# A two-layer decoder trunk on one core: the MLP in two phases, its down-projection in seven products

## The chip, the core and the metric

The kernel runs on one core of a Trainium2 chip. The core has a matrix engine (TensorE, PE in the profile; its weight loads are PEld), three engines for elementwise work (VectorE or DVE, ScalarE or ACT, GpSimd or POOL), and DMA queues that SyncE (SP) and ScalarE issue to. Data lie in DRAM, in SBUF (128 partitions) and in PSUM, where matmuls accumulate: eight banks of 128 x 512 floats. The metric is the device time of one execution in microseconds (us); lower is better.

## The reference

Two layers on a sequence of T = 1024 tokens and D = 1024 channels in float32. Layer 0 mixes tokens with dilated attention and a gated convolution, layer 1 with retention; each layer ends in a gated MLP of inner width 2816:

```python
def conv_glu_ffn(xn, w_up, conv_w, w_down):
    u = causal_dwconv(xn @ w_up, conv_w)      # width 3, over tokens; w_up: [1024, 5632]
    g, val = jnp.split(u, 2, axis=-1)
    return (jax.nn.silu(g) * val) @ w_down    # [2816, 1024]
...
x = x + conv_glu_ffn(rms_norm(x, ffn_norm[l]), ffn_w_up[l], ffn_conv_w[l], ffn_w_down[l])
```

## The kernel before

**Precision.** A matmul operand is split into two rounded parts, hi and lo (`split`, L99: ACT casts hi, then POOL or DVE subtracts lo = src - hi), and a product is three passes (`PASSES`): hi*hi, hi*lo, lo*hi. A tile `hl` holds a split weight block of 128 x 512; there are HL = 6 of them, and RAW = 3 buffers `raw` for blocks as loaded.

**The residual stream** `xb` stays in SBUF, token tile by token tile (8 tiles of 128 tokens). The normed, transposed input of a projection is `xc`: seven split tiles (three blocks and four combinations of blocks) that the seven-product scheme needs.

**Up-projection.** `strassen` (L200) computes two column blocks of 128, a gate block and its value block, with the Strassen-Winograd scheme: seven products of 12 matmuls (4 K tiles x 3 passes) of 512 columns instead of eight. The products accumulate in the `b` banks; ACT and DVE add them into `u1` and `u2`. Weight sums s1 to s4 are made by DVE (L237, L238) and POOL (L239, L258). POOL makes the lo parts of all seven weights.

**The MLP loop.** `ffn` goes over 22 blocks j. After the seven products of block j, `conv` (L707) applies the width-3 convolution (ACT L717, four DVE operations L720), SiLU (L724) and the gate product (L725), and splits the result into `h`. Block j of `h` is then one K tile of the down-projection: `down` (through `sweep`, L282) multiplies it with a row block of w_down for all 8 token tiles and adds every output tile from an `o` bank to `xb` (L289, L294). The tables `MIX` and `LAST_MIX` say how many token tiles of the down-projection of block j - 1 go after each product of block j: the two kinds of product alternate on PE.

**The norm between phases.** `Norming.play` follows `PLAN`, a string of steps: a sweep of two token tiles (s), inverse rms (q), normed rows (r), transposes (t), combination into `xc` (c) for a pair of tiles, and products of the next projection's first block (h). After layer 0's MLP the sweeps of this plan are the down-projection of the last block, 48 matmuls. The first block after a norm works in two passes of 256 columns.

**What sets the order.** The code is written in an order of emission; a scheduler then places instructions on the engines' queues, and each engine runs its own queue in order and waits on semaphores.

Of the kernel before, what the change touches and what calls it, by code (L numbers as in the profile page):

```python
# [13 lines left out]
P = 128  # L14
# [15 lines left out]
PLAN = "s0 q0 s1 q1 r0 t0 s2 q2 c0 r1 t1 s3 q3 c1 r2 t2 c2 r3 h3 t3 c3 h4"  # L30
PLAN_LATE = "t0 c0 s2 q2 t1 s3 q3 c1 r2 t2 c2 r3 t3 h3 c3 h4"
# [7 lines left out]
PAIRS = ((0, 2), (1, 3), (4, 6), (5, 7))  # L39
ORDER = tuple(t for p in PAIRS for t in p)  # L40
# [3 lines left out]
def _constants():  # L44
    """Arrays that depend on the shapes alone."""
# [23 lines left out]
def trunk(tc, a):  # L69
# [29 lines left out]
    def split(hi, lo, src, eng=None):  # L99
        """src = hi + lo, both rounded to float32r"""  # L100
        act.copy(hi, src)  # L101
        (eng or pool).tensor_tensor(lo, src, f(hi), ALU.subtract)  # L102
# [39 lines left out]
    def rsqrt_mean(out, ss, n, width):  # L142
        """out = (ss / n + EPS) ** -0.5"""
# [3 lines left out]
    def row_gains(g, parts):  # L147
        """A gain of the D channels on every partition, in two halves."""
# [11 lines left out]
    def normed(xt, r, g, xn):  # L160
        """xn = xt * r * g"""
# [5 lines left out]
    def turn(xn, h, bank):  # L167
        """Four of the eight [128, 128] blocks of xn, transposed."""
# [29 lines left out]
    def strassen(w, c1, c2, xc, fp, banks, out, spare=None):  # L198
# [16 lines left out]
        def half(u, i):  # L215
            return u.rearrange("p (a b t) -> p a b t", a=2, b=2)[:, ps_ : ps_ + 2 // np_, i, :]
# [13 lines left out]
        for n, bank in enumerate(banks):  # L230
            cols_, ps_ = slice(n * width, (n + 1) * width), n
            if n == 0:
# [8 lines left out]
                weights(12, a12)  # L241
                u1, u2 = fp.tile([P, T], "u", 4), fp.tile([P, T], "u", 4)
# [60 lines left out]
    # =============================== layer 0: even mixer ===============================  # L303
# [57 lines left out]
    def natural(w, c0, half, banks):  # L361
        """banks[t] = xnorm[tokens of tile 4*half + t] @ w[:, c0:c0+512]"""
# [655 lines left out]
```

## Time and profile before

| | |
|---|---|
| time, median of 3 runs | 2870.95 us (2869.23 to 2872.1) |
| span of the profiled execution | 2866.6 us; its own time is not given, the runs' median is 4.35 us longer than this span |
| busy | PE 2760.7 us (96%), DVE 1810.0 (63%), POOL 1552.6 (54%), ACT 1101.8 (38%) |
| DMA | 210.84 MB, 74 GB/s on average |

The span is the time from the first to the last instruction on the core. Busy time is a sum over instructions; matmuls overlap each other, so the duration of one in a list (some 395 ns) is longer than the distance between two. The chain of work that ended last shows those distances. "Idle before" and an arrow name what an engine waited for.

### The profile page before, as it was taken

Reading aid. Unit: us, or ns where it says so; the run is one execution under the profiler, and the core shown is the slowest. Engines: PE = TensorE matmul, PEld = TensorE weight load, DVE = VectorE, ACT = ScalarE, POOL = GpSimd, SP = SyncE. Lnnn points to the kernel's source line nnn. Section 1 sums busy time; section 2 is a strip of 40 time slices with the busy share of each in tenths; the row PEclk is TensorE's granted clock in tenths of the full one; section 3 lists DMA queues with packets and bytes.
Section 4 is the critical chain, followed back from the end, with each engine's and each line's share of the span. In section 5 each row is a group of like instructions: output and inputs, shape, how many; then the busy total and the mean of one; then the engine's idle time right before and its main releaser. Section 6 shows DMA issues by size and latency. Waiting matters only on the chain.

```text
span 2866.6 us, 34181 instructions
## 1 busy us (share of the span) xinstructions
PE 2760.7 (96%) x12513; PEld 2229.6 (78%) x12513; DVE 1810.0 (63%) x2670; ACT 1101.8 (38%) x1860; POOL 1552.6 (54%) x1185
## 2 busy tenths in 40 slices
PE   8999999789999999978999999999997999999998
PEld 6877777677888888867888877788876888888887
DVE  4256665876776776785222224888777767767767
ACT  4344443343343343343333333323334343343342
POOL 6711113356566566555666665555556666566563
PEclk9999999899999999988999999999999999999999
DMA  4310002011111111103333335444221111111112
GB/s 152 103 43 25 21 32 82 22 57 52 55 48 52 56 48 49 59 22 96 111 101 112 111 99 190 150 143 151 88 74 53 48 49 55 49 51 56 49 52 77
DMA packets 214988, 210.84 MB, mean 74 GB/s; under 512 B 10368, under 2 KB 162340, under 8 KB 214820
## 3 DMA queue, kind: packets, MB, share of 16 engines
q1 hardware_dynamic: 207900, 183.49, 20.1%
q10 hardware_dynamic: 6920, 25.17, 2.3%
q8 instruction: 98, 1.61, 0.2%
q14 instruction: 70, 0.57, 0.1%
HBM read 179.26 MB, written 29.36 MB: 73 GB/s over the span
## 4 chain that ended last, share of the span: by engine, by line
PE 79%; DVE 10%; POOL 4%; issue 3%; DMA 2%; ACT 1%; SPq 0%; ACTq 0%; POOLq 0%; DVEq 0%
PE b L210 43%; PE o L289 18%; PE u L419 5%; PE n L368 2%; PE u L368 2%; PE s L457 2%; POOL hl L102 2%; DVE xb L294 2%; PE pv L485 1%; PE u L289 1%; DVE u L164 1%; PE pt L497 1%; DMA raw<-in_ret_wo 1%; DVE s L800 1%; PE b L171 1%
## 5 line engine op out<-in xcount | busy, mean ns | idle before, releaser
L210 PE MATMUL b<-xc,hl 128*128 128x512 f32 (+1 forms) x5676 | 1331.9, 393 | 6.1 <-DVE xc L102 2.8
L210 PEld LDWEIGHTS b<-xc,hl 128*128 128x128 f32 x5676 | 1056.3, 189 | 259.9 <-DVE xc L102 3.6
L102 POOL TENSOR_TENSOR hl<-raw,hl 128x512 fp32r<-128x512 f32 x435 | 576.8, 1332 | 881.8 <-ACT hl L101 846.0
L294 DVE TENSOR_TENSOR xb<-xb,o 128x512 f32<-128x512 f32 x880 | 571.3, 682 | 304.8 <-PE o L289 301.8
L101 ACT CAST hl<-raw 128x512 fp32r<-128x512 f32 x444 | 274.2, 619 | 794.5 <-issue 288.1
L289 PE MATMUL o<-hl,h 128*128 128x512 f32 x2112 | 520.6, 398 | 14.3 <-DVE xb L294 10.5
L289 PEld LDWEIGHTS o<-hl,h 128*128 128x128 f32 x2112 | 400.1, 190 | 113.0 <-DVE xb L294 15.0
L102 POOL TENSOR_TENSOR hl<-s,hl 128x512 fp32r<-128x512 f32 x260 | 408.0, 1570 | 108.1 <-ACT hl L101 107.8
L720 DVE SCALAR_TENSOR_TENSOR u<-u,cc,u 128x1023 f32<-128x1023 f32 (+3 forms) x184 | 289.2, 1580 | 7.9 <-ACT u L717 5.0
L101 ACT CAST hl<-s 128x512 fp32r<-128x512 f32 x269 | 165.7, 618 | 88.4 <-PE b L210 40.2
L271 DVE TENSOR_TENSOR u<-u,b 128x512 f32<-128x512 f32 (+1 forms) x68 | 45.9, 675 | 212.5 <-issue 190.5
L419 PE MATMUL u<-xT,hl 128*128 128x512 f32 x576 | 164.5, 408 | 0.0
L237 DVE TENSOR_TENSOR s<-raw,raw 128x512 f32<-128x512 f32 x68 | 54.4, 800 | 130.9 <-DMA raw<-in_ffn_w_up 35.0
L258 POOL TENSOR_TENSOR s<-raw,s 128x512 f32<-128x512 f32 x65 | 124.9, 1921 | 5.1
L717 ACT ACTIVATE u<-u,cc 128x1024 f32<-128x1024 f32 (+1 forms) x92 | 102.0, 1115 | 56.7 <-DVE u L273 31.7
L239 POOL TENSOR_TENSOR s<-raw,raw 128x512 f32<-128x512 f32 x65 | 89.0, 1370 | 51.4 <-DMA raw<-in_ffn_w_up 43.6
L419 PEld LDWEIGHTS u<-xT,hl 128*128 128x128 f32 x576 | 99.2, 189 | 21.8 <-issue 5.8
L102 POOL TENSOR_TENSOR h<-u,h 128x512 fp32r<-128x512 f32 x84 | 106.6, 1288 | 0.0
L289 PE MATMUL o<-hl,ya 128*128 128x512 f32 x384 | 98.0, 406 | 3.7 <-DVE xb L294 3.7
L289 PEld LDWEIGHTS o<-hl,ya 128*128 128x128 f32 x384 | 73.2, 193 | 21.4 <-DVE xb L294 4.6
L725 DVE TENSOR_TENSOR u<-u,u 128x1024 f32<-128x1024 f32 (+1 forms) x46 | 56.2, 1222 | 50.5 <-ACT u L724 50.5
L102 POOL TENSOR_TENSOR xc<-u,xc 128x512 fp32r<-128x512 f32 x48 | 67.8, 1442 | 36.5 <-ACT xc L101 33.1
(183 smaller groups left out, 3078.2 us busy)
## 6 DMA issues: line engine op xcount, KB each, us to landing
raw<-in_ffn_w_up SPq DMA_DIRECT2D x176, 256.0 KB, 2.8
scr<-u ACTq DMA_DIRECT2D x48, 512.0 KB, 4.2
raw<-in_ffn_w_down SPq DMA_DIRECT2D x88, 256.0 KB, 2.6
raw<-in_even_w_in SPq DMA_DIRECT2D x72, 256.0 KB, 2.8
raw<-in_ret_wo SPq DMA_DIRECT2D x64, 256.0 KB, 2.6
xb<-in_x SPq DMA_DIRECT2D x16, 512.0 KB, 5.0
raw<-in_ret_wv SPq DMA_DIRECT2D x32, 256.0 KB, 4.1
raw<-in_ret_wg SPq DMA_DIRECT2D x32, 256.0 KB, 3.3
```

The source lines that it names most:

```text
L101: act.copy(hi, src)
L102: (eng or pool).tensor_tensor(lo, src, f(hi), ALU.subtract)
L210: pe.matmul(u, hl[:, ws, k * P : (k + 1) * P], xc[b][:, xs, k, cols_], start=(first and k == 0 and i == 0), stop=(k == 3 and i == 2), skip ...
L239: helper.tensor_tensor(s3, a11, a21, ALU.subtract)
L258: helper.tensor_tensor(s4, a12, s2, ALU.subtract)
L289: pe.matmul(o, lhs[j](ls, t), ws[j][hf][:, w, :], start=(j == 0 and i == 0), stop=(j == n - 1 and i == 2),)
L294: dve.tensor_tensor(xs, xs, o, ALU.add)
L368: pe.matmul(banks[t], xT[:, xs, k, t0 : t0 + P], hl[:, ws, :], start=(k == 0 and i == 0), stop=(k == KT - 1 and i == 2),)
L419: pe.matmul(u, hl(ws, k), xT[:, xs, k, hf * 512 : (hf + 1) * 512], start=(k == 0 and i == 0), stop=(k == KT - 1 and i == 2),)
L457: pe.matmul(sp[:, :n], qk[h0 : h0 + 64, 0, qs, i * P : (i + 1) * P], qk[h0 : h0 + 64, 1, ks, k0 : k0 + n], start=(j == 0), stop=(j == 2),)
L717: act.mul(c[:, t0:t1], u[:, t0:t1], wcol(2, jj))
L720: dve.scalar_tensor_tensor(c[:, s0:t1], u[:, s0 - d : t1 - d], wcol(2 - d, jj), c[:, s0:t1], ALU.mult, ALU.add)
```

## The change

The MLP becomes two phases. In the first the 22 blocks of the up-projection follow each other without products of the down-projection between them; `conv` leaves its result unsplit, and ACT's queue stores it to a DRAM tensor `hs`. In the second, `down_steps` computes the down-projection as Strassen-Winograd on tokens x inner width x channels, each halved: seven products of 11 K tiles x 4 token tiles x 3 passes. Their accumulators are the four `o` banks (x) and the four `b` banks (y). Six stages of 11 steps follow each other:

- stage 1: h11 x w11 into x, which is then added to the left half of tiles 0 to 3 and kept;
- stage 2: h12 x w21 into y;
- stage 3: two products of sums (s1, t1 into y, s2, t2 onto x), 24 matmuls a step; POOL also makes h11 - h21;
- stage 4: two more (s4 x w22 onto y, (h11 - h21) x t3 onto x), 24 matmuls a step;
- stage 5: h22 x t4 onto half of x, 6 matmuls a step; t4 is also stored to DRAM (`ts`);
- stage 6: the other half of the same product, 6 matmuls a step, from `ts` and `hs`; the norm that follows runs beside stages 5 and 6 (`PLAN_DOWN`).

Blocks of h come back from `hs`, are kept in `q` tiles in the space of `xc`, and are split anew in the phase (POOL or DVE). `RAW` becomes 5, `HL` 7, the norm's gains get two buffers `g` of their own, and retention's token halves become 0 to 511 and 512 to 1023 (`lay=1`, `PAIRS[1]`).

```diff
-RAW = 3
-HL = 6
+RAW = 5
+HL = 7
+KH = NFF // 2
+AHEAD = 3
+PLAN_DOWN = (
+    "a0 d2 a1 d2 a2 d2 a3 d5 A0 A1 b0 b1 B0 B1",
+    "d3 t0 c0 d3 t1 c1 d3 h1 d2 b2 A2 B2 b3 h1 t2 c2 h2 A3 B3 t3 c3 h4",
+)
-MIX = (0, 0, 0, 0, 3, 3, 2)
-LAST_MIX = (0, 0, 0, 0, 3, 0, 0)
...
+            if space is None:
+                kw["reuse_waits"] = "tile"
...
-            self.g = row_gains(g, [wk.tile([P, HALF], "s", 3) for _ in range(2)])
+            self.g = row_gains(g, [wk.tile([P, HALF], "g", 2) for _ in range(2)])
...
+    def down_steps(w):
...
+        def plain(k, l, r):
+            return [(hilo(l), hilo(r, None, dve))]
...
+        def load_56(k):
+            q["22", k] = lhs(1, 1, k)
+            r = u_tile()
+            sync.dma_start(out=r, in_=w[k * P : (k + 1) * P, :])
+            return lhs(1, 0, k, raw()), q["22", k], r[:, :HALF], r[:, HALF:], rhs(1, 1, k)
+
+        def make_56(k, a21, a22, b11, b12, b22):
+            s1, t1 = add(s_tile(), a21, a22, ALU.add), add(s_tile(), b12, b11, ALU.subtract)
+            p5 = hilo(s1), hilo(t1)
+            q["s2", k] = s2 = add(tile(), s1, q["11", k], ALU.subtract)
+            q["t2", k] = t2 = add(tile(), b22, t1, ALU.subtract)
+            add(q["11", k], q["11", k], a21, ALU.subtract, pool)
+            return [p5, (hilo(s2, None, dve), hilo(t2, None, dve))]
...
+        def make_37(k, b22, b12):
+            s4, t3 = add(q["12", k], q["12", k], q["s2", k], ALU.subtract), add(s_tile(), b22, b12, ALU.subtract)
+            return [(hilo(s4, None, dve), hilo(b22)), (hilo(q["11", k]), hilo(t3, None, dve))]
...
+        def make_4(k, b21):
+            t4 = add(q["t2", k], b21, q["t2", k], ALU.subtract)
+            r = quarter(q["22", k][:, :256]), hilo(t4, None, dve)
+            act.dma_start(out=ts[k], in_=t4)
+            return [r]
+
+        def load_4b(k):
+            t4, a22 = raw(), raw()
+            sync.dma_start(out=t4, in_=ts[k])
+            sync.dma_start(out=a22[:, :256], in_=hs[KH + k, :, HALF + 256 : T])
+            return t4, a22
...
+        groups = (
+            (load_1, plain, [(x, four, True)], lambda: evict(x, 0, 0)),
+            (load_2, plain, [(y, four, True)], lambda: evict(y, 0, 0)),
+            (load_56, make_56, [(y, four, True), (x, four, False)], lambda: (evict(y, 4, 1), evict(x, 0, 1))),
+            (load_37, make_37, [(y, four, False), (x, four, False)], lambda: (evict(y, 0, 1), evict(x, 4, 1))),
+            (load_4, make_4, [(x[:2], two, False)], lambda: evict(x[:2], 4, 0)),
+            (load_4b, make_4b, [(x[2:], two, False)], lambda: evict(x[2:], 6, 0)),
+        )
...
+        for j in range(NFF):
...
+            for n, _ in enumerate(steps):
+                if n == 2:
+                    store()
+                if j == NFF - 1 and n >= 1:
+                    if n == 1:
+                        close_xc(0, 1)
+                        d.append(down_steps(w_down))
+                    advance(1)
...
+            held.append((j, conv(j, us)))
+        advance(4)
+        store()
+        tail(until, d[0])
...
+    def to_ret(until, down):
+        until(4)
+        nrm = Norming(a["odd_norm"][0:1], 1)
+        nrm.play(PLAN_DOWN[0], sweep=down)
+        open_xc()
...
+        nrm.play(PLAN_DOWN[1], nxt["xc"], down, nxt["head"][0])
```

Where instructions stand, before and now (the number at a name's end is its buffer's). First PE, inside the MLP of layer 0, in a block of the up-projection; `b` are the seven products' banks, `o` the down-projection's. Before, from the fourth product of a block to the end of the block:

```order
L210 MATMUL b_6973<-xc_4914,hl_7006 128x512 x12
L210 MATMUL b_6976<-xc_4913,hl_7021 128x512 x12
L289 MATMUL o_7058<-hl_6943,h_6928 128x512 x3
L289 MATMUL o_7063<-hl_6948,h_6928 128x512 x3
...
L289 MATMUL o_7083<-hl_6948,h_6928 128x512 x3
L210 MATMUL b_6973<-xc_4915,hl_7039 128x512 x12
L289 MATMUL o_7103<-hl_6943,h_6928 128x512 x3
```

Now, the same place and the next block's start:

```order
L218 MATMUL b_6254<-xc_4916,hl_6287 128x512 x12
L218 MATMUL b_6257<-xc_4915,hl_6302 128x512 x12
L218 MATMUL b_6254<-xc_4917,hl_6321 128x512 x12
L218 MATMUL b_6257<-xc_4914,hl_6337 128x512 x12
L218 MATMUL b_6400<-xc_4912,hl_6380 128x512 x12
```

The 48 matmuls of the down-projection have left the block, and the seven products of one block stand directly before those of the next.

Then DVE in stage 3 of the down-projection (layer 0), about one step; `q` are kept blocks, `s` sums, L741 is `add`, L109 the lo part of a split:

```order
L741 TENSOR_TENSOR s_9254<-raw_9111,q_9107 128x512
L109 TENSOR_TENSOR hl_9174<-q_9168,hl_9174 128x512
L741 TENSOR_TENSOR q_9264<-s_9254,q_8580 128x512
L741 TENSOR_TENSOR s_9256<-u_9109 128x512
L741 TENSOR_TENSOR q_8830<-q_8830,q_9264 128x512
L741 TENSOR_TENSOR q_9266<-raw_9113,s_9256 128x512
L109 TENSOR_TENSOR hl_9216<-q_9211,hl_9216 128x512
```

Before, what DVE did for the down-projection was the addition of its tiles to `xb`, between the convolution's steps:

```order
L294 TENSOR_TENSOR xb_71<-xb_71,o_7843 128x512
L294 TENSOR_TENSOR xb_71<-xb_71,o_7848 128x512
L720 SCALAR_TENSOR_TENSOR u_7887<-u_7692,cc_5382,u_7887 128x1023
L720 SCALAR_TENSOR_TENSOR u_7887<-u_7692,cc_5382,u_7887 128x1022
L276 TENSOR_TENSOR u_7691<-u_7691,b_7696 128x2x256
```

Seven operations a step on SBUF operands alone have come (the fifth is stage 4's s4, which the scheduler has moved into stage 3), and the 16 additions from PSUM per block are gone; four per group of banks remain at the stages' ends.

Last PE at the end of layer 0's MLP, where the norm lies. Now, the end of stage 6 and the first products of retention (128 x 128 are the norm's transposes):

```order
L806 MATMUL o_8487<-hl_10645,hl_10642 128x512 x2
L806 MATMUL o_8488<-hl_10645,hl_10642 128x512 x2
L218 MATMUL o_10714<-xc_10449,hl_10662 128x256 x12
L178 MATMUL b_10734<-ident_67,u_10700 128x128 x4
L218 MATMUL o_10715<-xc_10450,hl_10677 128x256 x2
L218 MATMUL o_10716<-xc_10455,hl_10731 128x256 x2
```

Before, the last sweeps and the transposes of the first pairs:

```order
L289 MATMUL o_10661<-hl_10563,hl_10479 128x512 x3
L289 MATMUL o_10666<-hl_10568,hl_10479 128x512 x3
L289 MATMUL o_10671<-hl_10563,hl_10479 128x512 x3
L289 MATMUL o_10676<-hl_10568,hl_10479 128x512 x2
L171 MATMUL b_10641<-ident_67,u_10635 128x128 x4
L289 MATMUL o_10676<-hl_10568,hl_10479 128x512
L171 MATMUL b_10646<-ident_67,u_10638 128x128 x4
```

Before, all four pairs of tiles were turned among or behind the last 48 matmuls; now two pairs are turned beside stage 6, and when its last matmul has gone the first block's products stand next, with the transposes of the last two pairs among them.

More of the change, by code (lines that the diff above doesn't have):

```diff
@@ L730, in down @@
-        def down(j, h, tiles, after=None):
-            def lhs(s, t):
-                return h[t // 4][:, s, t % 4 * P : (t % 4 + 1) * P]
-            return sweep([lhs], [w_rows(w_down, j)], tiles, o_bank, after)
-        d = iter(())
+            for jj, u, c in ((NFF + j, us[1], cs[1]), (j, us[0], cs[0])):
+                act.mul(c, u, wcol(2, jj))
+                for d in (1, 2):
+                    dve.scalar_tensor_tensor(c[:, d:], u[:, :-d], wcol(2 - d, jj), c[:, d:], ALU.mult, ALU.add)
@@ new lines, in conv, with store, advance, until @@
+            act.activation(cs[0], cs[0], AF.Silu)
+            dve.tensor_tensor(cs[0], cs[0], cs[1], ALU.mult)
+            return cs[0]
+        held = []
+        def store():
+            for j, h in held:
+                act.dma_start(out=hs[j], in_=h)
+            held.clear()
+        done = [0]
+        def advance(n):
+            for _ in range(n):
+                next(d[0])
+            done[0] += n
+        def until(g):
+            advance(2 * AHEAD + g * KH - done[0])
+        d = []
@@ L984, in trunk, with to_out, put @@
     nrm.play(PLAN_LATE, xc, wo_sweep(half, h, yT, 1, ORDER[4:]), head[0])
[L987 to L991 removed]
+    def to_out(until, down):
+        def put(t, cs=slice(0, D)):
+            sync.dma_start(out=a["out"][0, t * P : (t + 1) * P, cs], in_=xb[:, t, cs])
+        until(4)
+        next(down)
+        next(down)
+        for t in range(4):
+            put(t)
+            next(down)
+        for t in (6, 7):
+            put(t, slice(HALF, D))
+        for _ in range(5):
+            next(down)
+        next(down)
+        next(down)
+        for t in (4, 5):
+            put(t)
+        run(down)
+        for t in (6, 7):
+            put(t, slice(0, HALF))
+    ffn(1, xc, head, 0, to_out)
     for p in (ps, dp, wk, mp, sm, xp, wp, cp):
```

167 lines of the change are left out of this document (108 added, 59 removed).

## The prediction

> **What bounds the kernel now.** I read the page first (engine totals, then the chain that ended last), then the chain in order of time around one MLP block and around the two ends of the MLPs, then the table of windows by stage, and last the timeline of one block for VectorE (DVE) and GpSimd (POOL).
>
> ```profile
> span 2866.6 us, 34181 instructions
> ...
> PE 79%; DVE 10%; POOL 4%; issue 3%; DMA 2%; ACT 1%; SPq 0%; ACTq 0%; POOLq 0%; DVEq 0%
> PE b L210 43%; PE o L289 18%; PE u L419 5%; PE n L368 2%; PE u L368 2%; PE s L457 2%; POOL hl L102 2%; DVE xb L294 2%; PE pv L485 1%; PE u L289 1%; DVE u L164 1%; PE pt L497 1%; DMA raw<-in_ret_wo 1%; DVE s L800 1%; PE b L171 1%
> ```
>
> TensorE (PE) is 79% of the chain, and its two largest lines are those that the change touches: L210, the seven-product projections, and L289, which in the MLPs is the down-projection. Now the price of a matmul, from one MLP block (chain in order of time: start, length, what) and one windowed table (us, PE, PEld, DVE, ACT, POOL busy with counts, clock, DMA share, GB/s):
>
> ```profile
> 1161.23 14.04 PE b L210 x60
> 1175.27 4.18 PE o L289 x18
> 1179.45 2.81 PE b L210 x12
> 1182.26 4.18 PE o L289 x18
> 1186.45 2.81 PE b L210 x12
> 1189.26 2.78 PE o L289 x12
> 1192.04 14.04 PE b L210 x60
> ```
> ```profile
> 0.00:36.00 36.00, 22.58 (x107) 17.42 (x107) 25.19 (x32) 22.59 (x41) 19.02 (x28) 1.00 0.59 202
> 650.00:1235.00 585.00, 584.72 (x2505) 471.15 (x2505) 413.94 (x513) 223.83 (x341) 365.58 (x248) 1.00 0.17 53
> 1235.00:1320.00 85.00, 61.99 (x301) 51.84 (x300) 75.70 (x105) 39.47 (x73) 39.73 (x40) 0.80 0.07 22
> 1320.00:1680.00 360.00, 359.73 (x1567) 290.35 (x1566) 90.08 (x112) 128.22 (x216) 221.62 (x165) 1.00 0.33 110
> ```
>
> A block is 84 + 48 = 132 matmuls of 512 columns in 1192.04 - 1161.23 = 30.81 us, so 0.2334 us each, without a hole, and PE is busy 584.72 of 585 us. Within a block only fewer matmuls can help. Retention's projections (1320 to 1680) run the same seven products with no down-projection between them, as the changed MLP will; the copies of L261 there come once a block:
>
> ```profile
> 1693.42 0.59 ACT L261 COPY u<-b 128x512 f32<-128x512 f32 x1 [0.73 <-PE b L210]
> ...
> 1752.46 0.59 ACT L261 COPY u<-b 128x512 f32<-128x512 f32 x1 [0.78 <-PE b L210]
> ```
>
> Three blocks lie between these two rows: 59.04 / 3 = 19.68 us for 84 matmuls, 0.2343 each. The holes are at the MLPs' ends:
>
> ```profile
> 1246.73 0.69 DVE u L276
> 1247.42 4.63 DVE u L720 x7
> ...
> 1254.57 5.25 PE o L289 x12
> ...
> 1292.29 2.83 PE b L171 x12
> ...
> 1318.84 345.91 PE b L210 x1512
> ...
> 2837.58 0.69 DVE u L276
> 2838.27 4.63 DVE u L720 x7
> ...
> 2845.42 16.73 PE o L289 x63
> ...
> 2862.17 0.69 DVE xb L294
> ```
>
> In layer 0, from the last up-product's end at 1246.7 to 1318.84, PE has 78 matmuls of the down-projection (18.2), 64 transposes (2.83 / 12 = 0.236 each, 15.1) and retention's first block, 168 of 256 columns (84 x 0.2343 = 19.7): 53.0 of 72.1 us, so 19.1 are idle. In layer 1, from 2837.6 to 2862.2, 78 matmuls take 18.2 of 24.6: 6.4 idle.
>
> **The resource that the change leans on.** It moves work to DVE and POOL. The timeline of one block shows how these two meet:
>
> ```profile
> 844.05 0.69 DVE L294 TENSOR_TENSOR xb<-xb,o 128x512 f32<-128x512 f32 x1
> 844.10 1.29 POOL L102 TENSOR_TENSOR hl<-raw,hl 128x512 fp32r<-128x512 f32 x1 [2.38 <-ACT hl L101]
> 848.36 2.60 DVE L720 SCALAR_TENSOR_TENSOR u<-u,cc,u 128x1023 f32<-128x1023 f32 x2
> 851.47 2.47 DVE L294 TENSOR_TENSOR xb<-xb,o 128x512 f32<-128x512 f32 x4
> 853.33 1.31 POOL L102 TENSOR_TENSOR hl<-raw,hl 128x512 fp32r<-128x512 f32 x1 [0.94 <-ACT hl L101]
> 853.86 4.09 DVE L720 SCALAR_TENSOR_TENSOR u<-u,cc,u 128x1023 f32<-128x1023 f32 x2
> 854.59 2.29 POOL L102 TENSOR_TENSOR hl<-s,hl 128x512 fp32r<-128x512 f32 x1
> 857.17 1.94 POOL L102 TENSOR_TENSOR hl<-s,hl 128x512 fp32r<-128x512 f32 x1 [0.30 <-ACT hl L101]
> 859.14 1.23 DVE L725 TENSOR_TENSOR u<-u,u 128x1024 f32<-128x1024 f32 x1 [1.19 <-ACT u L724]
> 859.19 2.34 POOL L258 TENSOR_TENSOR s<-raw,s 128x512 f32<-128x512 f32 x1
> ```
>
> A POOL subtraction takes 1.29 us, beside a DVE add with one operand in PSUM too (844.05). Beside a DVE operation with both operands in SBUF the two take turns: the pair of L720 grows from 2.60 to 4.09, POOL's splits from 1.29 to 2.29 and 1.94, L258 to 2.34. From 853.86 to 859.11 two of each fill 5.25 us, and 2 x 1.30 + 2 x 1.29 = 5.18: one at a time, no gain from overlap. Freed at 857.95, POOL ends at 859.11: 1.16 us of its own; the rest, 5.25 - 2 x 1.16 = 2.93 less some 0.8 of waiting at 853.86 for the split of 853.33, leaves 1.08 per 1023 elements of DVE, so about 0.55 for 512.
>
> The Trainium skill says this of all such pairs ("SBUF — State Buffer", section "Who interferes with whom"): a DVE instruction with two SBUF inputs and a GpSimd instruction that reads SBUF exclude each other, while one SBUF input does not collide. The rows agree in both halves. Without that rule the busiest new stage would be free (DVE 4.2, POOL 3.9 of 5.6 us a step) and the sum 20 us lower; with it, the stage is bound by the pair, as below.
>
> **The change, part by part.** (a) Fewer matmuls. The down-projection had 22 x 8 x 2 x 3 = 1056 per layer; seven products of 11 x 4 x 3 = 132 are 924. 264 fewer in all, x 0.2334 = -61.6 us, all on the path.
>
> (b) Up-projection alone: a block has 19.7 us instead of 30.8. In SBUF-SBUF turns it needs POOL's seven splits and two combinations, 9 x 1.16 = 10.4, and DVE's four convolution steps, gating product and two sums, 4 x 1.08 + 1.1 + 1.1 = 6.5: 16.9 of 19.7, where before it was 13 x 1.16 + 6.5 = 21.6 of 30.8. POOL's part alone is hidden in retention (19.68). The convolution is new there, and the next block's first copy waits for a u buffer that it frees. Between nothing and 0.5 us a block (42 blocks: 0 to 21); DVE's 6.5 of turns plus five PSUM operations of 0.60 fit, so I take 0.15: +6. ScalarE's new store of h replaces two casts (one issue for two instructions), the four up loads per block are retention's, and 512 KB more per 19.7 us is 27 GB/s: hidden by the same cover.
>
> (c) Stages 1 and 2 (11 steps of 12 matmuls, 2.80 us): one POOL split, one DVE split, 1.16 + 0.55 = 1.7 of 2.8. Loads 512 KB a step, 187 GB/s, under the 202 of the first window. Free; the switch from the last block and the shared accumulators between the stages cost an eviction each (0.69 us, L276's row): 2.5 us a layer, +5.
>
> (d) Stage 3 (11 steps of 24, 5.60 us): by the order of instructions DVE has seven SBUF-SBUF operations a step (four sums and differences, two splits, and the difference s4 of stage 4 pulled forward), POOL three: 7 x 0.55 + 3 x 1.16 = 7.3 against 5.6. Over 11 steps 80 against 61.6. Ahead of the stage stand some 15 of DVE's and 4 of POOL's, 12 us, done in the slack of stage 2; 68 - 61.6 = 7, and 3 for handing over. Bounds 0 (more done ahead) and 19 (nothing ahead); I take 10 a layer: +20.
>
> (e) Stage 4: 3 x 0.55 + 2 x 1.16 + a difference t4 0.55 = 4.5 of 5.6: free. Stages 5 and 6 (1.40 us a step): 0.55 + about 0.65 for POOL's half-width split fit, but stage 6 takes two raw buffers a step out of five; a buffer is held for the landing, a cast and a split, about 2.8 + 0.6 + 0.7 = 4.1 us by the page's median for these weights, so 1.64 a step. In layer 1 +3.
>
> ```profile
> raw<-in_ffn_w_up SPq DMA_DIRECT2D x176, 256.0 KB, 2.8
> ```
>
> (f) The ends. The last convolution now lies beside stage 1, which needs only the first eleven blocks of h: 6.4 in layer 1 go. In layer 0, 5 of the 19.1 are that bubble; the norm's 14 get 132 matmuls of cover (30.8 us) instead of 48. What stays: after the last product, evict, square, rms, rows, transposes, combination for tiles 6 and 7, some 16 us by such rows as 0.69 and 2.83, under 9.8 us of first products and 3.8 of transposes; and the pair's turns in stages 5 and 6, about 40 us for 38 of PE. I leave 10 of 19.1: -9. Together -15, with the half clock's share in it (0.80 in that window). The final eviction and store after 2862.2 stay.
>
> (g) Elsewhere: five raw buffers for three, seven split ones for six, and gains in their own buffers at the two other norms. Between 0 and -8; -3.
>
> Sum: -61.6 + 6 + 5 + 20 + 3 - 15 - 3 = -45.6. Against the profiled execution: 2866.6 - 45.6 = 2821.0. The runs' median, 2870.95, is 4.35 above that span; with it 2825.4. I forecast 2826.
>
> **The rivals.** Pair of DVE and POOL not binding: enough of stage 3 is prepared ahead, and the ends close fully. For it: stage 2 leaves 1.1 us of turns a step. Against: seven split buffers hold less than two steps. 20 + about 4 less: 2802.
>
> DMA binds the down phase. A layer moves about 42 MB in 216 us (88 blocks of w_down, 44 of h, 11 of t4 out and back, each 262 KB, and half blocks of h), 194 GB/s on average; stage 3 moves 1.3 MB in 5.6 us, 234, which is above every window read here (202 at a share of 0.59). For it: nothing here ran at 234. Against: the share, 0.59, leaves room to 342. If 190 were the limit, stage 3 would take 76 instead of 72 and stages 5 and 6 some 6 more, 10 a layer: 2846.
>
> Slower: the convolution's turns stall the up-projection. If each of its four steps waits for one POOL split, 4 x (1.08 + 1.16) = 9.0 us after the last product, the next block's first copy misses the fourth product's start at 36 x 0.234 = 8.4, and each block waits. Without term (b) the sum is -51.6, so it decides from 51.6 / 42 = 1.2 us a block; at 2 us the time is 2903. For it: 853.86 shows such waits. Against: at 84 instead of 132 matmuls POOL still has 9 splits a block, a whole block's lead, and retention shows no hole.
>
> **Chances.** Forecast (2806 to 2848): 0.62. Not binding, under 2806: 0.10. DMA or a costlier down phase, 2848 to 2865: 0.14. Stalled up-projection, 2865 and over: 0.14, of which 0.04 within 0.2% (5.7 us, about what a measurement of this kernel can tell from no change) and 0.10 slower. Faster: 0.86. Range 2800 to 2864.
>
> **What would show it.** L806 (down) with 1848 matmuls where L289 had 2112 for h; L261's copies 19.7 to 20.0 us apart in the MLPs; stage 3 about 72 us with POOL and DVE durations swollen and PE waiting for hl; no hole after the last convolution. Wrong if blocks are over 21 us apart, if PE waits for raw loads through the down phase, or if stage 3 takes 62.

## The result and the profile after

The changed kernel takes 2882.82 us (median of 4 runs, 2881.68 to 2885.68) against 2870.09 us: a ratio of 1.0053, interval 1.0039 to 1.0067. It is slower by half a per cent, where 2826 us was forecast. The profiled execution took 2885.68 us, its span is 2883.9 us, 17.3 us longer than the span before.

First the page of the changed kernel: span, busy time, and the chain that ended last by engine and by line.

```profile
span 2883.9 us, 34447 instructions
...
PE 2727.5 (95%) x12249; PEld 2175.7 (75%) x12249; DVE 1770.4 (61%) x2342; ACT 1179.1 (41%) x2030; POOL 1611.0 (56%) x1207
...
PE 45%; POOL 23%; issue 16%; DVE 11%; DMA 3%; ACT 2%; POOLq 0%; SPq 0%; ACTq 0%; DVEq 0%
PE b L218 17%; POOL hl L109 15%; PE o L806 5%; PE u L431 5%; PE b L806 3%; POOL s L249 3%; PE n L380 2%; PE s L469 2%; PE u L380 2%; POOL s L270 2%; PE o L301 2%; DVE xb L306 1%; PE pv L497 1%; PE u L301 1%; DVE hl L109 1%
```

PE's share of the chain has fallen from 79% to 45%, POOL's has risen from 4% to 23%. PE is still busy for 95% of the span: the helpers lead it by little, but they lead. The 16% of "issue" are time for which the profile shows no wait; in the MLP's blocks it is mostly POOL's idle time, looked at below. Next the program cut at its stages (windows: us, then PE, PEld, DVE, ACT, POOL busy with counts, clock, DMA share, GB/s). For the kernel before: layer 0's 21 full-width blocks of the MLP, what follows up to retention's first full-width product, layer 1's 21 blocks.

```profile
600.39:1246.70 646.31, 641.83 (x2744) 515.86 (x2744) 451.98 (x557) 247.92 (x378) 401.33 (x269) 1.00 0.17 52
1246.70:1327.20 80.50, 57.49 (x310) 49.59 (x310) 71.87 (x101) 41.48 (x79) 43.52 (x42) 0.79 0.10 30
2191.53:2837.55 646.02, 641.84 (x2744) 515.82 (x2744) 452.06 (x557) 246.56 (x378) 399.95 (x269) 1.00 0.16 51
```

For the changed kernel, layer 0: the 21 blocks, stages 1 to 6 of the down-projection, what follows up to retention's first full-width product; then layer 1's blocks and its stages 3 and 6.

```profile
596.35:1036.05 439.70, 424.02 (x1766) 329.07 (x1766) 293.79 (x235) 196.16 (x297) 306.54 (x185) 1.00 0.26 82
1036.05:1065.97 29.92, 29.92 (x134) 24.78 (x132) 19.26 (x19) 14.62 (x24) 15.63 (x11) 1.00 0.89 306
1065.97:1102.44 36.47, 30.40 (x133) 24.53 (x132) 25.07 (x28) 13.71 (x24) 21.09 (x15) 0.95 0.44 146
1102.44:1182.96 80.52, 68.55 (x265) 53.04 (x266) 68.47 (x76) 23.93 (x42) 45.81 (x30) 0.92 0.37 121
1182.96:1247.12 64.16, 60.73 (x265) 49.23 (x264) 34.38 (x50) 26.61 (x49) 31.54 (x26) 1.00 0.50 160
1247.12:1264.27 17.15, 15.58 (x67) 12.25 (x67) 14.66 (x18) 11.57 (x25) 13.25 (x16) 1.00 0.02 8
1264.27:1291.10 26.83, 21.78 (x101) 16.77 (x100) 22.84 (x32) 19.02 (x39) 21.16 (x21) 0.94 0.48 138
1291.10:1329.72 38.62, 29.91 (x200) 27.09 (x200) 27.70 (x41) 19.39 (x39) 25.10 (x20) 0.87 0.29 82
...
2193.32:2632.00 438.68, 423.75 (x1766) 329.15 (x1766) 293.74 (x235) 194.85 (x296) 306.53 (x185) 1.00 0.26 82
...
2698.38:2778.37 79.99, 69.35 (x265) 53.57 (x265) 68.98 (x76) 23.92 (x42) 45.99 (x30) 0.91 0.37 121
...
2858.58:2880.05 21.47, 18.94 (x67) 11.20 (x65) 9.09 (x13) 8.35 (x18) 6.61 (x9) 1.00 0.61 196
```

At retention's price of 19.68 us, 21 blocks are 413.3 us; they took 439.7 and 438.7. Stage 3 should be 264 x 0.2334 = 61.6 us and took 80.5 and 80.0. Stage 2 lost 5.7 us, stage 6 11 us in layer 0 (part of it the norm's own PE work) and 6 us in layer 1. Stage 1, whose loads are the densest of these windows (306 GB/s), lost nothing.

**The block.** One block of the changed kernel's timeline (start, length, engine, line; in brackets the idle time before it and what ended it), from one sum s1 of the weights (L247) to the next:

```profile
806.46 1.75 DVE L247 TENSOR_TENSOR s<-raw,raw 128x512 f32<-128x512 f32 x1 [5.54 <-POOL s L270]
...
808.14 0.67 DVE L283 TENSOR_TENSOR u<-u,b 128x512 f32<-128x512 f32 x1
...
808.85 0.59 ACT L284 COPY u<-b 128x512 f32<-128x512 f32 x1 [3.10 <-DVE u L283]
809.46 0.69 DVE L285 TENSOR_TENSOR u<-u,b 128x512 f32<-128x512 f32 x1
...
810.19 2.20 ACT L872 ACTIVATE u<-u,cc 128x1024 f32<-128x1024 f32 x2 [0.76 <-DVE u L285]
811.37 6.92 DVE L874 SCALAR_TENSOR_TENSOR u<-u,cc,u 128x1023 f32<-128x1023 f32 x4 [0.62 <-ACT u L872]
812.29 0.60 ACT L108 CAST hl<-s 128x512 fp32r<-128x512 f32 x1
...
812.97 2.04 POOL L109 TENSOR_TENSOR hl<-s,hl 128x512 fp32r<-128x512 f32 x1 [5.30 <-ACT hl L108]
...
816.17 0.59 ACT L257 COPY u<-b 128x512 f32<-128x512 f32 x1 [2.75 <-DVE u L874]
...
816.81 14.49 PE L218 MATMUL b<-xc,hl 128*128 128x512 f32 x59 [0.53 <-ACT u L257]
...
818.39 1.06 ACT L875 ACTIVATE u<-u 128x1024 f32<-128x1024 f32 x1 [1.12 <-DVE u L874]
819.36 0.61 ACT L108 CAST hl<-raw 128x512 fp32r<-128x512 f32 x1
...
825.99 1.29 POOL L270 TENSOR_TENSOR s<-raw,s 128x512 f32<-128x512 f32 x1
...
827.31 1.77 DVE L247 TENSOR_TENSOR s<-raw,raw 128x512 f32<-128x512 f32 x1 [5.53 <-POOL s L270]
```

There are three buffers for the sums of weights, and a block makes four sums. The next block's s1 takes the buffer of this block's s2, whose last reader is s4 (L270), near the end of POOL's work for this block. DVE does its instructions in order and stands 5.5 us at s1. Behind it stand the additions that empty the current block's product banks (L283, L285). ScalarE's copy (L284) and multiplication (L872) wait for these, and only behind them does ScalarE cast (L108) what POOL splits next; POOL has been idle for 5.30 us by then. The convolution's steps on DVE (L874) come later still, and ScalarE's SiLU (L875), which waits for them, stands ahead of further casts. So POOL's splits come late, its s4 comes late, and so round again: a loop over three engines of 20.87 us. All blocks of a layer take about this long but the first (23.5 us in layer 0, 22.8 in layer 1) and the last (19.68).

**Stage 2's end.** Timeline of the changed kernel again, for DVE and then for PE:

```profile
1083.41 0.68 DVE L741 TENSOR_TENSOR q<-s,q 128x512 f32<-128x512 f32 x1
...
1084.73 1.79 DVE L109 TENSOR_TENSOR hl<-raw,hl 128x512 fp32r<-128x512 f32 x1
...
1096.69 0.69 DVE L741 TENSOR_TENSOR q<-raw,s 128x512 f32<-128x512 f32 x1
...
1099.95 1.75 DVE L109 TENSOR_TENSOR hl<-q,hl 128x512 fp32r<-128x512 f32 x1
1101.62 0.68 DVE L814 TENSOR_TENSOR xb<-xb,b 128x512 f32<-128x512 f32 x1
```
```profile
1093.76 2.81 PE L806 MATMUL b<-hl,hl 128*128 128x512 f32 x11 [0.20 <-DVE hl L109]
1102.44 1.62 PE L806 MATMUL b<-hl,hl 128*128 128x512 f32 x3 [5.87 <-DVE xb L814]
```

Stage 2's last product ends at 1096.6, but the first addition that empties its accumulators stands behind what DVE prepares for stage 3 (from 1096.69 on, among others) and starts at 1101.62; stage 3's first product goes into those accumulators. The first two rows also show the turns: the same size of DVE operation takes 0.68 us alone and 1.79 us while POOL works.

### The profile page after: what moved, and what is told of

It is laid out like the page before. It is cut to its first block, busy times and chain, and to the rows that moved or that the text cites. A ratio compares the mean times of both kernels' runs of the same rounds, so it can differ in the third digit from the quotient of the medians.

```text
span 2883.9 us, 34447 instructions
## 1 busy us (share of the span) xinstructions
PE 2727.5 (95%) x12249; PEld 2175.7 (75%) x12249; DVE 1770.4 (61%) x2342; ACT 1179.1 (41%) x2030; POOL 1611.0 (56%) x1207
## 4 chain that ended last, share of the span: by engine, by line
PE 45%; POOL 23%; issue 16%; DVE 11%; DMA 3%; ACT 2%; POOLq 0%; SPq 0%; ACTq 0%; DVEq 0%
PE b L218 17%; POOL hl L109 15%; PE o L806 5%; PE u L431 5%; PE b L806 3%; POOL s L249 3%; PE n L380 2%; PE s L469 2%; PE u L380 2%; POOL s L270 2%; PE o L301 2%; DVE xb L306 1%; PE pv L497 1%; PE u L301 1%; DVE hl L109 1%
## 5 line engine op out<-in xcount | busy, mean ns | idle before, releaser
L218 PE MATMUL b<-xc,hl 128*128 128x512 f32 (+1 forms) x5676 | 1330.6, 394 | 34.2 <-ACT u L257 22.8
L109 POOL TENSOR_TENSOR hl<-raw,hl 128x512 fp32r<-128x512 f32 (+1 forms) x391 | 578.9, 1499 | 505.4 <-ACT hl L108 464.6
L109 POOL TENSOR_TENSOR hl<-s,hl 128x512 fp32r<-128x512 f32 x304 | 431.3, 1428 | 399.8 <-ACT hl L108 399.8
L108 ACT CAST hl<-raw 128x512 fp32r<-128x512 f32 (+1 forms) x466 | 280.7, 610 | 411.0 <-PE o L301 80.9
L247 DVE TENSOR_TENSOR s<-raw,raw 128x512 f32<-128x512 f32 x68 | 114.0, 1677 | 473.6 <-POOL s L270 472.5
L874 DVE SCALAR_TENSOR_TENSOR u<-u,cc,u 128x1022 f32<-128x1022 f32 (+1 forms) x176 | 304.9, 1789 | 26.5 <-ACT u L872 26.3
L806 PE MATMUL o<-hl,hl 128*128 128x512 f32 x1056 | 273.1, 409 | 37.2 <-DVE hl L109 30.5
L108 ACT CAST hl<-s 128x512 fp32r<-128x512 f32 x335 | 207.2, 620 | 227.1 <-POOL hl L109 65.9
L806 PEld LDWEIGHTS o<-hl,hl 128*128 128x128 f32 x1056 | 203.6, 196 | 96.4 <-DVE hl L109 44.3
L806 PE MATMUL b<-hl,hl 128*128 128x512 f32 x792 | 192.6, 395 | 13.1 <-DVE xb L814 12.5
L806 PEld LDWEIGHTS b<-hl,hl 128*128 128x128 f32 x792 | 150.4, 191 | 48.3 <-issue 12.6
L109 POOL TENSOR_TENSOR hl<-q,hl 128x512 fp32r<-128x512 f32 (+1 forms) x88 | 116.5, 1329 | 82.1 <-ACT hl L108 79.1
L108 ACT CAST hl<-q 128x512 fp32r<-128x512 f32 (+1 forms) x176 | 101.4, 590 | 70.3 <-PE b L806 34.7
L306 DVE TENSOR_TENSOR xb<-xb,o 128x512 f32<-128x512 f32 x176 | 115.1, 679 | 21.7 <-PE o L301 21.4
L284 ACT COPY u<-b 128x512 f32<-128x512 f32 (+1 forms) x68 | 39.3, 578 | 187.3 <-DVE u L283 186.8
L872 ACT ACTIVATE u<-u,cc 128x1024 f32<-128x1024 f32 x88 | 97.1, 1146 | 33.2 <-DVE u L285 31.7
L109 DVE TENSOR_TENSOR hl<-raw,hl 128x512 fp32r<-128x512 f32 x75 | 65.8, 884 | 61.5 <-ACT hl L108 59.0
```

The costliest lines, as they stand in the source:

```text
L218: pe.matmul(u, hl[:, ws, k * P : (k + 1) * P], xc[b][:, xs, k, cols_], start=(first and k == 0 and i == 0), stop=(k == 3 and i == 2), skip ...
L247: dve.tensor_tensor(s1, a21, a22, ALU.add)
L306: dve.tensor_tensor(xs, xs, o, ALU.add)
L806: pe.matmul(o, l[:, ls, c * P : (c + 1) * P], r[:, ws, :], start=(start and i == 0), stop=(stop and i == 2), skip_group_check=True,)
L872: act.mul(c, u, wcol(2, jj))
L874: dve.scalar_tensor_tensor(c[:, d:], u[:, :-d], wcol(2 - d, jj), c[:, d:], ALU.mult, ALU.add)
```

## The experiments

The kernel before was run again beside the experiments, and each ratio below is to these runs. It took 2868.53 us beside the first four (the three on the up-projection and the first on stage 3), 2867.74 beside the next four (one operation of stage 3, the work on DVE in the kernel before, both shifts, and the paired loads), and 2868.27 beside the last four.

### The up-projection: which buffer, and whose work

Theory A: the loop through the three sum buffers. Rival B: the u buffers, which the convolution frees late (the prediction's reason). A third run takes POOL out of the block.

```
-            return fp.tile([P, 512], "s", 3)
+            return fp.tile([P, 512], "s", 4)      # up_s4, and the other "s" tiles of SBUF
```


> Four s tiles instead of three, nothing else. In the changed kernel a block of the up-projection takes 20.87 us instead of 19.68, and DVE waits 5.5 us a block at the first weight sum (L247) for POOL's s4 (L270). Theory A, too few s tiles: the sum of a later block waits for a tile that POOL frees last, and the evictions and the convolution stand behind it on DVE; then a block falls to 19.7 to 19.9 us and the kernel by about 42 x 1.1 = 46 us, to 2837. Theory B, too few u tiles (the first copy of a block, L257, waits for the convolution): the wait at L247 goes but a block stays at 20.6 to 20.9. Theory C, DVE and POOL taking turns fill the block: it stays at 20.8.

```
-RAW = 5
+RAW = 4
...
-                u1, u2 = fp.tile([P, T], "u", 4), fp.tile([P, T], "u", 4)
+                u1, u2 = fp.tile([P, T], "u", 5), fp.tile([P, T], "u", 5)   # up_u5
```


> Five u tiles instead of four (and four raw buffers instead of five, for the space). Theory B, the first copy waits for a u tile that the convolution frees: a block falls to 19.7 us, the kernel by 42 x 1.15 = 48 us. Theory A, s tiles: the copy no longer waits, but the loop over POOL's s4, DVE's sum and the x evictions stays: 20.3 to 20.9 us a block, 0 to 20 us less. Theory C: 20.8. The down phase may lose some us by the fourth raw buffer less (stage 6, two raw buffers a step).

```
-        helper = pool if np_ == 1 else dve
+        helper = dve                              # up_dve
```


> All of POOL's work in the seven-product projections of full width (seven lo parts, two combinations per block) goes to DVE, in the MLPs and in retention's projections. Theory C, turns: without POOL there are none, DVE has 9 x 0.60 + 6.5 + 5 x 0.60 = 14.9 of 19.7 us, so a block takes 19.7 to 19.9: about 46 us less. Theory A: the same, since DVE frees its own s tiles. If DVE's queue itself is the trouble (everything in order behind sums that wait): longer than 20.87, up to 22, and retention's blocks grow from 19.68 as well.

Measured: four sum buffers 2837.70 us, ratio 0.9892 (0.9876 to 0.9909); five u buffers 2897.4 us, 1.0102 (1.0087 to 1.0117); POOL's work on DVE 2819.4 us, 0.983 (0.9815 to 0.9844). One block each as a window, of the changed kernel, of the one with four sum buffers and of the one with the work on DVE:

```profile
821.00:841.87 20.87, 20.20 (x86) 15.66 (x85) 14.07 (x12) 9.23 (x14) 14.98 (x10) 1.00 0.25 78
```
```profile
809.20:828.88 19.68, 19.68 (x86) 15.82 (x85) 13.07 (x11) 9.54 (x15) 15.50 (x10) 1.00 0.26 81
```
```profile
804.00:823.68 19.68, 19.68 (x86) 15.82 (x85) 15.54 (x20) 9.66 (x15) 0.00 (x0) 1.00 0.25 77
```

The second row settles it. POOL is as busy as ever (15.50 us), turns and all, and the block is down to 19.68 with PE never idle. Nor does the length of the convolution by itself make the block late: with four sum buffers its steps on DVE are stretched even more, 7.97 us for four against 6.92.

```profile
818.07 7.97 DVE L874 SCALAR_TENSOR_TENSOR u<-u,cc,u 128x1023 f32<-128x1023 f32 x4
```

One buffer of 2 KB per partition is worth 42 us in the two stretches of 21 blocks, 416.79 and 419.47 us instead of 439.70 and 438.68; the other 3 of the 45 us are sums and differences elsewhere, since the edit reaches all "s" tiles. The u buffers are not it: with five of them the rows of L273, whose copies come once a block, still lie 62.6 / 3 = 20.87 apart:

```profile
L273 ACT COPY u<-b x4: 586/586/587, 800.4 to 863.0; 128x512 f32<-128x512 f32 x4
```

The 14.6 us that this run lost lie in the down-projection: over both layers stages 3, 4 and 6 grew by 6 to 7 us each. The raw buffer given up is the likely reason, but stage 3 uses u tiles too, and no run separates the two. Moving the work to DVE opens the loop at its other end (s4 is then DVE's own, done in order). It gained 18 us more than the fourth buffer. The first block of each MLP took 19.8 us where it still takes 23.2 and 25.9 with four buffers; the two stages 4 took 63.8 and 62.9 us where that kernel has 70.0 and 65.6, and the retention's projections and rows (what lies between the projections and the MLP) 455.8 and 398.7 us where it has 458.3 and 403.5.

### Stage 3: turns, or a late handover

```
-            p5 = hilo(s1), hilo(t1)
+            p5 = hilo(s1, None, dve), hilo(t1, None, dve)
...
-            add(q["11", k], q["11", k], a21, ALU.subtract, pool)
+            add(q["11", k], q["11", k], a21, ALU.subtract)      # dn_dve: both; dn_h11: this line alone
```


> In stage 3 of the down-projection POOL's three operations a step (two lo parts and h11 - h21) go to DVE. Turns bind stage 3 (7 x 0.55 + 3 x 1.16 = 7.3 us a step, 80 measured): then 10 x 0.60 = 6.0 a step, stage 3 falls from 80 to 66 to 70 us in each layer, 20 to 28 us less in all. If loads bind it (1.3 MB a step): 80 as before. If DVE's own queue binds it: as with turns' 66, or longer by the evictions, 72. Stage 2's hole of 6.3 us, where the eviction of the y banks stands behind DVE's work for stage 3, would stay or grow by 1 or 2.

> The changed kernel with one of stage 3's three POOL operations moved to VectorE, h11 - h21, whose result is not read before stage 4. Theory A, turns on the shared port: a step of 7.3 us loses POOL's 1.16 and gains VectorE's 0.55, so 6.7 us, 11 steps 73.6 us instead of 80; with stage 2's hole some 3 us smaller the kernel is near 2882.8 - 2 x 9 = 2864 us. Theory B, latency: stage 3 waits for the low halves of product 5's factors because POOL hands them over late; the moved operation is not in that chain, so stage 3 stays at 80 and the kernel at 2883 us. Theory C, POOL's queue alone: three operations become two, a third of POOL's part of the step is gone (1.16 us a step), stage 3 is 67 us and the kernel near 2852 us.

Measured: all three operations on DVE 2836.71 us, 0.9888 (0.9873 to 0.9903), 46 us less where 20 to 28 were expected; the one difference alone 2870.05 us, 1.0005 (0.9996 to 1.0015). Layer 0's stages 2 and 3 as windows, with three moved and with one:

```profile
1066.58:1096.50 29.92, 29.92 (x133) 24.77 (x132) 19.89 (x28) 12.56 (x22) 11.20 (x9) 1.00 0.46 147
1096.50:1159.45 62.95, 60.46 (x265) 49.38 (x264) 62.82 (x105) 25.11 (x44) 2.61 (x2) 1.00 0.50 169
```
```profile
1066.18:1101.97 35.79, 30.40 (x133) 24.54 (x132) 25.67 (x31) 13.70 (x24) 17.74 (x13) 1.00 0.47 151
1101.97:1176.54 74.57, 66.45 (x265) 52.28 (x265) 71.73 (x85) 23.91 (x42) 30.92 (x20) 0.93 0.39 130
```

Stage 3 went 80.5, 74.6, 63.0 us with three, two and no operations on POOL. The theory of turns gave 80 and 73.6 for the first two; a late handover would have left the second at 80, POOL's queue alone would have made it 67. So it is the pair. That DVE should take over work in a stage where it is already the busier one (68.5 of 80.5 us) and the stage get shorter by 17 us looks odd until one sees what its busy time held: in the second row 105 operations fill 62.82 us, 0.60 each; in the changed kernel 76 filled 68.47, 0.90 each, swollen by POOL's turns.

The gain of 46 us is more than stage 3 accounts for (17.6 and 17.0 us), because the wait at stage 2's end shrank too, where it was expected to stay or grow: DVE, no longer held off, reaches the evictions sooner. PE still waits 2.5 us behind the first matmul of stage 3, 1.5 of them for a split and 1.0 for the eviction. With one operation moved stage 2 still lost 5.0 us (35.79 less 30.8) instead of some 3 less than 5.7, and stage 3 took 74.6 and 75.1 us; so that run came out 6 us above its 2864.

### Was POOL's work too much before the change already?

The line of up_dve, in the kernel before.

> The kernel before with the full-width seven-product projections' POOL work on VectorE. If the turns bind only where the up-projection runs alone: MLP blocks stay at 30.78 us and retention's projections at 19.6 us; the rows around them may give a few us as they did in the changed kernel (6.5 + 2.5 us in the retention there), so 2860 to 2869 us. Rival: POOL's work binds in the kernel before too, and the shift is worth as much there as in the changed kernel: 2810 us or less. On the other side: VectorE also carries the down-projection's work there, and becomes late: above 2875 us.

Measured: 2872.36 us, 1.0015 (1.0006 to 1.0025), 3 us beyond the range expected and if anything slower; blocks of the MLP are near 31.0 us instead of 30.81. With 48 more matmuls in a block nothing in the loop is late. The gain of moving this work exists only since the change took that cover away.

### The two shifts together, and what is left

> Both shifts from POOL to VectorE together: the full-width up-projections' POOL work and stage 3's three POOL operations. If each shift acts in its own stage (turns between VectorE and POOL, up-projection and stage 3 apart): 2819.4 for the first alone less the 46.1 us that the second took from the changed kernel (2882.8 to 2836.7), so 2773 us, 2768 to 2780; blocks 19.68 us, stage 3 near 63 us, stage 2 near 30. Rival: VectorE, now with the work of both, becomes the bound where the last block meets the first steps of the down-projection, and gives back 15 us or more: 2788 or above.

Measured: 2773.51 us, ratio 0.9673 (0.9659 to 0.9688), on the expected 2773. This kernel is called both_dve below. The page:

```profile
span 2772.8 us, 33953 instructions
...
PE 77%; DVE 10%; POOL 5%; issue 3%; DMA 2%; ACT 2%; SPq 0%; ACTq 0%; DVEq 0%; POOLq 0%
```

PE has 77% of the chain again (79% before the change). The two effects add, so they are two, each in its own stage. Five more runs went after the rest, each as an edit of this kernel.

Stage 6, by fewer raw buffers: a22's quarter for two steps in one buffer.
```
-            t4, a22 = raw(), raw()
+            t4 = raw()
...
+            if k % 2 == 0:
...
+                q["22b"] = raw().rearrange("p (a t) -> p a t", a=2)     # both_pair: loads two steps' quarters
```


> As both_dve, and stage 6 loads the last token quarter of h22 for two steps into one raw buffer, so 11 + 6 = 17 raw buffers are filled in stage 6 instead of 22. If the cycle through the 5 raw buffers sets stage 6 (26.8 us in layer 0, 20 to 21 in layer 1): 17/22 of it, 20.7 and 16 us, 8 to 12 us less than both_dve in all. Rival: the way of t4 through DRAM or the norm's work on VectorE and ScalarE set it, and it stays within 2 us of both_dve.

Measured: 2772.25 us, 0.9668 (0.9654 to 0.9683), the same as without. Layer 0's stage 6 stayed (28.1, now 28.3 us), layer 1's went from 20.6 to 18.9, where 16 was expected. The cycle through the raw buffers is a small part in layer 1 and nothing in layer 0.

Stage 6, with nothing of the norm beside it:
```
-    "d3 t0 c0 d3 t1 c1 d3 h1 d2 b2 A2 B2 b3 h1 t2 c2 h2 A3 B3 t3 c3 h4",
+    "d9 d2 t0 c0 t1 c1 h1 b2 A2 B2 b3 h1 t2 c2 h2 A3 B3 t3 c3 h4",      # norm_after
```


> As both_dve, but in layer 0 all steps of stage 6 are issued ahead of the norm's transposes, combinations and first products, which stood between them. Theory A, the norm's work slows stage 6 in layer 0 (28.1 us there, 20.6 us in layer 1, where no such work stands beside it): stage 6 falls to about 21 us, and the 35.4 us from its end to the first full-width product grow by what was done beside it, two pairs' transposes and combinations, by an estimate of 15 us: 2773.5 - 7 + 15 = 2781 us. Theory B, stage 6 is set by its own loads and splits: it stays near 28 us, and the kernel is at 2788 us or above. On the other side, if the overlap costs more than it hides: 2770 us or less.

Measured: 2779.38 us, 0.9692 (0.9677 to 0.9706), 6 us above both_dve. Stage 6 and the stretch behind it, first with the norm beside it, then without:

```profile
1213.75:1241.84 28.09, 23.30 (x100) 18.38 (x99) 24.46 (x32) 19.13 (x39) 21.61 (x21) 0.85 0.48 144
1241.84:1277.31 35.47, 28.39 (x200) 26.14 (x200) 33.03 (x51) 20.48 (x41) 14.27 (x12) 0.93 0.29 84
```
```profile
1213.51:1234.77 21.26, 18.82 (x80) 14.58 (x79) 13.06 (x18) 10.95 (x23) 9.15 (x13) 0.92 0.64 189
1234.77:1284.27 49.50, 34.39 (x221) 30.34 (x220) 44.15 (x65) 29.09 (x57) 25.58 (x20) 0.83 0.21 61
```

Stage 6 falls by 6.8 us and the stretch behind it grows by 14.0: the norm beside the last product slows that product, and still hides 7 us more than it costs.

The border of stages 2 and 3: the other product of the step first.
```
-            return [p5, (hilo(s2, None, dve), hilo(t2, None, dve))]
+            return [(hilo(s2, None, dve), hilo(t2, None, dve)), p5]
...
-            (load_56, make_56, [(y, four, True), (x, four, False)], ...
+            (load_56, make_56, [(x, four, False), (y, four, True)], ...     # swap
```


> As both_dve, with the two products of a stage-3 step in the other order: first the one summed into the banks that need no eviction, then the one that must wait for stage 2's eviction. If TensorE's wait at the border of stages 2 and 3 (2.5 us a layer in the kernel with stage 3 on VectorE, 6.3 in the changed kernel) is for that eviction behind VectorE's prepared work: 12 matmuls, 2.8 us, now cover it, and 2 x 2.5 = 5 us go: 2768.5 us. Rival: the first step's factors themselves are late, and those of the product now first are the later ones: the wait stays or grows, 2773 to 2780 us.

Measured: 2772.59 us, 0.9665 (0.965 to 0.9679); stage 3 62.9 us as before. The wait behind the first matmul is still 1.5 us, for a split on DVE, and 0.8 us remain for the eviction, where both_dve has 1.5 and 1.0. Both_dve's trace shows why there was little to gain: the scheduler had put six matmuls of that product first already.

POOL's other work on DVE, in the down-projection and the combinations, and then in every split:
```
-            return [(hilo(l), hilo(r, None, dve))]
+            return [(hilo(l, None, dve), hilo(r, None, dve))]   # down_all: so too in make_37, quarter and combine
```
```
-        (eng or pool).tensor_tensor(lo, src, f(hi), ALU.subtract)
+        dve.tensor_tensor(lo, src, f(hi), ALU.subtract)         # split_all
```


> As both_dve, with all POOL work of the down-projection and of the combinations for the next norms on VectorE. Theory A, turns: a POOL operation holds VectorE off for longer than VectorE would need to do it (1.16 against 0.55 us), so it is gained wherever VectorE has room: stage 4 (VectorE 45.6 of 65 us) near its 61.6 us of matmuls, stage 6 some 3 us shorter in each layer: 2773.5 - 4 - 6 = 2764 us. Theory B, VectorE becomes the bound after stage 6, where it is busy for 32.7 of 35 us already, and gets 16 more operations of 0.6 us for the four combinations: 10 us more there and less gained before, 2775 to 2785 us.

> As both_dve, with the low halves of every split of the kernel on VectorE, in the attention and the retention too. Where VectorE has room (attention 243 of 360 us busy) nothing changes, since TensorE is busy for 355 of 360 us. In the retention's rows (400 us; VectorE 331, POOL 218, TensorE 378 us) theory A, turns: POOL's 1.16 us become 0.55 us and VectorE is no longer held off, TensorE's 22 idle us shrink by some 5 to 10 us; with the down-projection's part as in the run with its POOL work moved, 2760 us. Theory B, VectorE's sum becomes the bound (331 plus half of POOL's 218 is 440 us for 400): 2800 us or above.

Measured: 2775.63 us, 0.9674 (0.9659 to 0.9688), and 2780.23 us, 0.9693 (0.9677 to 0.9709). The first falls in theory B's range, but by luck: the stretch behind stage 6, which theory B saw growing, went from 35.5 to 33.2 us, and the time can't be told from both_dve's. Stage 3 went to 61.8 and 61.0 us, but stage 4 stayed at 64.6, stage 6 of layer 0 grew to 30.8, and the retention's rows took 405.9 us instead of 400.1. The second met neither expectation. Retention's rows, of both_dve and of split_all:

```profile
1732.98:2133.08 400.10, 377.95 (x1899) 316.31 (x1898) 331.58 (x524) 146.69 (x262) 218.44 (x211) 0.97 0.36 117
```
```profile
1735.53:2138.64 403.11, 379.12 (x1898) 315.91 (x1898) 374.04 (x640) 146.20 (x262) 64.93 (x94) 0.97 0.35 116
```

116 operations more raised DVE by only 42.5 us, 0.37 each, less than 0.60, so the others must have shrunk, and yet nothing ended sooner. What PE's 22 idle us there hang on, no run shows. The shift pays where the pair of DVE and POOL is the bound, as in stage 3, and not as a rule. The best three, 2772.25 to 2773.51 us, cannot be told apart.

## Why the prediction was wrong

By its own terms, in us. "Measured" is worked out from windows of the two traces, those above, those of layer 1 and the stretches between, against matmuls at 0.2334 and blocks at 19.68.

| term | predicted | measured | from |
|---|---|---|---|
| (a) fewer matmuls | -61.6 | -61.6 | 1848 at L806 instead of 2112 |
| (b) up-projection alone | +6 | +42.6 | 439.7 + 438.7 - 2 x 413.3 = 51.8, less 9.2 that the blocks before exceeded their matmuls by (646.31 - 413.3 - 978 x 0.2334 = 4.7, and 4.5) |
| (c) stages 1, 2 | +5 | +9.5 | 29.92 + 36.47 - 61.6 = 4.8 a layer |
| (d) stage 3 | +20 | +37.3 | 18.9 and 18.4 |
| (e) stages 4, 5; 6 in layer 1 | +3 | +13.6 | 2.5 + 1.8; 1.9 + 1.3 + 6.1 |
| (f) ends | -15 | -19.3 | layer 0: 80.50 - 53.0 = 27.5 idle, now 26.83 + 38.62 - 50.2 = 15.2; layer 1: -7.0 |
| (g) elsewhere | -3 | -4.8 | -4.0 ahead of the first MLP, -0.7 in the retention |
| sum | -45.6 | +17.3 | spans: +17.3 |

- **(b) is the step that failed first**: 0.15 us a block against 1.19 (20.87 less 19.68), over twice its upper bound of 0.5. It added up the turns of a block, 16.9 us in 19.7, and found room. The room was there: with a fourth sum buffer the same turns fit with PE never idle. What it did not price was the order: who waits for whose buffer, and what stands behind the waiting instruction. The row that spoke for safety, retention's 19.68 us, has the same three buffers and the same POOL work, but no convolution in DVE's queue behind the late s1; that this makes the difference is argued, no run left the convolution out. Its sign of being wrong, blocks over 21 us apart, did not show; at 20.87 they lay outside the 19.7 to 20.0 that it expected.
- **Its slower rival had the size and not the place.** It put the break-even at 1.2 us a block, and 1.19 came. But it made the late u buffer the cause. The changed kernel does show that wait (L257 behind L874, 2.75 us); with five u buffers it went, and the block stayed at 20.87 us. The convolution's stretched steps (6.92 us for four) are a part of the loop; the wait that closes it is s1's for s4.
- **(d) failed on what stands in DVE's queue.** It took 7 x 0.55 + 3 x 1.16 = 7.3 us a step, 80 us for 11 steps, less 12 for work done ahead and plus 3 for the handover, taken as 61.6 + 10 = 71.6. Measured were 80.5 and 80.0, though work was done ahead. The window of layer 0 holds 30 POOL operations where eleven steps have 33, and 76 of DVE's where they have 77, and 8 of these are evictions (L814, 4.74 us in this window). So 68 and 30 operations took turns, some of them for stage 4: at the prediction's prices 68 x 0.55 + 30 x 1.16 = 72.2 us, close to its 71.6. By an estimate the rest is the evictions, 4.74 us, which it did not count as DVE's time in this stage, and 0.60 instead of 0.55 for an operation of DVE (62.82 / 105 in the run with POOL out of the stage), 3.4 us: 80.3 in all. No run separates these two. That 11 x 7.3 without any credit gives 80 as well is chance. The work ahead also held back stage 2's eviction, which is the 5.7 us in (c).
- **(c)**: "free" was right for stage 1 (29.92 us, at 306 GB/s) and wrong at stage 2's end, where one eviction was counted at 0.69 us as if it stood at the head of DVE's queue.
- **(e)** was sized too small: layer 1's stage 6 was put at 3 us from raw buffers; it lost 6.1, and in both_dve buffers account for 1.7 of it. What sets the other 4 to 5 us, and stage 4's 2 to 4, stays open.
- **(f)** was right in kind. The end of layer 0 had more to give than counted (27.5 idle us, since some of the first block's products lay behind the cut at 1318.84), and gave 12.
- **The rivals on transfers** did not come: stage 1 moved 306 GB/s with no hole, above the 234 that stage 3 would have needed. Nor did "pair not binding": stage 3 became shorter with each operation taken from POOL. The rule cited from the Trainium skill ("SBUF — State Buffer", section "Who interferes with whom") was the right one of the two ways to cost stage 3, and the runs with one and three operations moved are its test: 74.6 and 63.0 us.

(b), (d), (c) and (e) are 36.6 + 17.3 + 4.5 + 10.6 = 69.0 us of miss, the ends and the rest gave 6.1 back: 62.9 between the forecast's -45.6 and +17.3.

## What to carry to other kernels

When a change takes away work that covered the helpers, don't only compare each engine's sum with the new period; walk the ring of every buffer that is smaller than one round needs, and add up the loop through it, including what stands in order behind the instruction that waits. Where two engines exclude each other, work given to the slower one (1.16 us against 0.60) costs the faster one that time too, so in a stage that they bind, the work belongs on the faster one even if that looks fuller. Work prepared ahead shortens a stage only by what the next stage's preparations and the evictions in the same queue don't take back, and it can hold those evictions up.

## What was not expected of the hardware

- DVE operations of 512 columns on SBUF operands went from 0.68 us to between 1.67 and 1.79 beside POOL's; with POOL out of stage 3 they follow each other every 0.60 us. The "busy" of an engine in such a stage contains the other's turn: DVE's 68.47 us for 76 operations would have been 46 alone, by an estimate from 0.60 each.
- Matmuls of 128x512 came every 29.92 / 132 = 0.2267 us in stage 1, and in stage 2 where nothing held it up (29.92 us with stage 3's work on DVE), while the blocks' took 0.2334 and 0.2343. What makes the 3% stays open; by the shorter distance the losses of the stages in the table would be some 3% of their matmuls' time larger.
- 306 GB/s at a DMA share of 0.89 (stage 1) is half above the densest window read of the kernel before (202), with PE not held up.
